# Starting a two-block kernel with the values of unnormalized x, weight parts made ahead, bias rows spread in pieces

## The chip, the cores and the metric

The kernel runs on one core of a Trainium2 chip, as one program. The metric is the device time of one execution in microseconds. Three runs of the kernel before gave a median of 2781.17 us (2778.04 to 2782.7).

## What is computed

Two blocks follow each other on 256 tokens of width 1024, all in float32. The first is a hybrid mixer and a gated feed-forward network; the second has four layers (gated linear attention, a convolution, grouped attention, gated linear attention), each with modulation by two condition vectors and a feed-forward network. Only the first block's mixer is touched. Cut to what matters:

```
h = rmsnorm(x, norm1_w)          # x * rsqrt(mean(x*x) + eps) * norm1_w, per token
q, k, v, z, xbc, dt, gates = split(h @ w_in)
attn = windowed attention of q, k, v in three dilations, 24 heads,
       logits + a bias row per head (looked up by distance)
ssm  = state-space scan of conv(xbc), with dt and z, then a norm
h2   = (gate0 * (attn @ w_attn) + gate1 * (ssm @ w_ssm)) @ w_out
```

A norm multiplies every token by one number and every channel by another. The channel factor can be put on x before a projection and the token factor on its result.

## The kernel before, in words

Activations are kept with channels on the 128 partitions and tokens along the row. A matrix product in float32 is made of three faster ones (`mm3`, L453): each operand is split into a high part, a rounded copy, and a low part, the rest; high times high, high times low and low times high are added up in PSUM.

Weights come from one packed array in units (`Unit`, L424). A unit has parts of 128 x 1024 values, 512 KB each. For each part SP issues a load into `wraw` (three buffers), ScalarE casts it into `whi` and VectorE subtracts to `wlo` (five buffers each; both on L435). A unit of the values has four parts, a unit of keys, queries or the SSM two. `fm2` (L594) takes a unit and runs its 48 matmuls into one PSUM bank of the tag `pl` (three buffers); the tag `pa` has five.

The instructions are traced in the order of the Python code, and a scheduler of the framework orders each engine's queue when the program is built: an instruction that was traced later may be put earlier where it expects its inputs to be ready. Each queue then runs in that fixed order. `order(a, b)` adds an edge that keeps a behind b. SP, ScalarE and GpSimd issue the DMAs from their own queues.

The start (L1762 to 1770) warms TensorE on zeros, loads x in four pieces on the queues of SP and ScalarE, then the whole vector table (`vec`) and the constants (`cst`). `block1` (L889) then runs in this order: `norm_plain` (L538) sums the squares, makes the per-token factor (`rstd_of`, L488) and the scaled h in two parts; `head_bias` (L606) multiplies one-hots by the bias table, writes the rows to DRAM and returns `spread` (L622), which writes each row 128 times to `ud` in DRAM, in three DMAs of eight heads each on ScalarE's queue; `decays` (L629) makes the step sizes dt; `attention` (L669) makes values in three units, keys in six and, between the heads' pairs, queries in six (`proj`, L684). `spread` is called after the first unit of keys; `load_bias` (L701) reads each head's bias from `ud` over GpSimd's queue. `conditions` (L1772) loads the condition vectors and takes their silu, traced before the first logits. `ssd` (L782) runs the SSM in four groups; each takes five units by `fm2` (B and C, two of x, two of z), with a convolution (`conv`, L789) on VectorE between them.

Of the kernel before, what the change touches and what calls it, by code (L numbers as in the profile page):

```python
# [138 lines left out]
NVEC = _o  # L139

# [7 lines left out]
CSTS = [("ident", 128), ("ones", 128), ("tri", 128), ("cumf", 128), ("cumb", 128), ("maskf", 128), ("maskb", 64),  # L148
# [8 lines left out]
def _constants():  # L157
# [8 lines left out]
    put("ones", 1.0)  # L166
# [162 lines left out]
def tile_blocks(ctx: ExitStack, tc: tile.TileContext, x, cx, wpk, wmod, vecd, rowd, cstd, hotd, g2d, out,  # L329
# [58 lines left out]
    ident, ones = cc("ident"), cc("ones")  # L388
# [35 lines left out]
    class Unit:  # L424
        def __init__(self, name, i, after=()):
            off, self.kt, self.cw = plan[name][i]
            n = self.kt * self.cw
            self.parts = []
            last_unit[0] = self
            for h in range(n // 1024):  # L430
                raw = glob.tile([P, 1024], FT, name="wraw", tag="wraw", bufs=WRAW)
                self.dma = nc.sync.dma_start(raw, bass.AP(tensor=wpk.tensor, offset=wpk.offset + off + h * 1024, ap=[[n, P], [1, 1024]])).ins
                hi = glob.tile([P, 1024], FR, name="whi", tag="whi", bufs=WHI)
                lo = glob.tile([P, 1024], FR, name="wlo", tag="wlo", bufs=WHI)
                i = A.copy(hi, raw).ins, V.tensor_tensor(lo, raw, hi, op=OP.subtract).ins  # L435
                for a, b in zip(i, after[h] if after and isinstance(after[0], tuple) else after):
                    if b is not None:
                        order(a, b)
                self.parts.append((hi, lo))
# [154 lines left out]
    def fm2(name, i, a, outer="f", after=()):  # L594


        w = Unit(name, i, after)
        ps = PL()
        order_ = [(k, f) for k in range(w.kt) for f in range(2)]
        if outer == "f":  # L600
            order_.sort(key=lambda x: x[1])
        for k, f in order_:
            mm3(ps, ps.t[:, f * 256:f * 256 + 256], w.at(k, f), a.at(k), k == w.kt - 1 and f == 1)
        return ps.t.rearrange("p (f t) -> p f t", f=2)

    def head_bias(pool):  # L606

        ud = dr.tile([24, P, BW], FT, name="ud")
        wide = []
        for g in range(N_DIL):  # L610
            hot = pool("hot", [33, BW])
            nc.sync.dma_start(hot, hotd[:, g * BW:(g + 1) * BW])
            o = VOFF["rel"][0] + g * HPG
            ps = PA()
            T.matmul(ps.t[0:HPG, :BW], vec[0:33, o:o + HPG], hot, start=True, stop=True)
            u = pool("u", [HPG, BW])
            order(A.copy(u, ps.t[0:HPG, :BW]).ins, norm_end[0])
            rows = dr.tile([HPG, BW], FT, name=f"rows{g}")
            nc.scalar.dma_start(rows, u)
            wide.append((ud[g * HPG:(g + 1) * HPG], rows))  # L620
# [8 lines left out]
    def decays(pool, h):  # L629

        w = Unit("dt", 0)
        ps = PL()
        for k in range(KD8):
            mm3(ps, ps.t[:, :256], w.at(k, 0), h.at(k), k == KD8 - 1)
        xd = glob.tile([32, 256], FT, name="xd")
# [33 lines left out]
    def attention(pool, h, ud, spread, ab, late):  # L669

        pool.tags(k=6, bt=4, L1=4, L0=4, P1=2, P0=2, dt=5)
        vt = [[O2([P, 512]) for _ in range(3)] for _ in range(2)]
        for i in range(3):
            w = Unit("v", i, () if i else norm_end)
            ps = [PL() for _ in range(2)]
            for k0 in range(0, KD8, 2):
                for t in range(2):
                    for k in (k0, k0 + 1):
                        mm3(ps[t], ps[t].t, h.at(k, t * P, P), w.row(k), k == KD8 - 1)
            for t in range(2):  # L680
                A.copy(vt[t][i], ps[t].t)
        kf, qf = [], []

        def proj(name, dst, i):  # L684
            ps = fm2(name, i, h)
            t = O2([P, 2, 256]) if name == "q" else pool(name, [P, 2, 256])
            A.copy(t, ps)
# [73 lines left out]
        conditions(lambda: pool("P1", [P, 512], pad=[P, 768]))  # L761
# [20 lines left out]
    def ssd(pool, h, lad, dt_tm, la_tm, ys):  # L782
# [22 lines left out]
        for g in range(SSM_G):  # L805
# [6 lines left out]
            conv(fm2(f"s{g}", 0, h), 0, bc, (16 + g, 20 + g))  # L812
            for i in range(2):
                conv(fm2(f"s{g}", 1 + i, h), 1 + i, xs[i], (g * 4 + 2 * i, g * 4 + 2 * i + 1))
            zt = []
            for i in range(2):
                ps = fm2(f"s{g}", 3 + i, h)
# [70 lines left out]

    def block1(early, final):  # L889
        with Pool("b1a") as pool:  # L890
            pool.tags(ct=10, hot=3, u=3)
            h = norm_plain(pool, lambda k: X[:, k, 0:256], "norm1", 256)
# [3 lines left out]
        with Pool("b1b") as pool:  # L896
            attention(pool, h, ud, spread, ab, late)
# [871 lines left out]
    nc.scalar.dma_start(vec, vecd[:, 0:NVEC])  # L1769
    nc.sync.dma_start(cst, cstd[:, 0:COFF["cos"][0]])  # L1770

    def conditions(th_):  # L1772

        o = ROFF["c"][0]
        nc.scalar.dma_start(cs.rearrange("p s d -> p (s d)"), bass.AP(tensor=rowd.tensor, offset=rowd.offset + o, ap=[[0, P], [1, 2 * D]]))
# [76 lines left out]
```

## Time and profile before

| | us |
|---|---|
| median of three runs | 2781.17 |
| the profiled execution | 2785.1 |
| its span | 2783.3 |
| TensorE busy | 2715.7 |
| VectorE busy | 2154.4 |
| ScalarE busy | 1275.4 |

The span is what the instruction records of the profiled execution cover; its own time is 1.8 us longer. PE is TensorE's matmuls, PEld its weight loads, DVE VectorE, ACT ScalarE, POOL GpSimd, SP the queue that issues loads; a name with a q, such as ACTq, is an engine's sequencer, which issues DMAs and waits. A row of the timeline gives the start, the length (from the first to the last of merged instructions), what it is with the tiles it writes and reads, and in brackets the idle time before it and what ended that.

### The profile page before, as it was taken

To read this page: it belongs to the slowest core of one execution; us is meant where nothing else is said; L and a number is where in the kernel's file an instruction comes from. 1 tells how busy PE (TensorE), PEld (TensorE's weight loads), DVE (VectorE), ACT (ScalarE), POOL (GpSimd) and SP (SyncE) were. 2 spreads that over 40 slices of the span, in tenths; PEclk is the share of its full clock that TensorE was granted. 3 is DMA by queue.
4 is the path that set the end of the run, shared out by engine and by line. 5 is a ranking of instruction groups with operands and counts; after the bars stand their busy time and mean duration, and the time that the engine had idled before them with its cause. 6 is when DMAs were issued, how large, how long until landed. Compare 5 with 4: busy or idle time off the path is not lost. (4 is left out here: it accounts for less than half of the span.)

```text
span 2783.3 us, 44045 instructions
## 1 busy us (share of the span) xinstructions
PE 2715.7 (98%) x17170; PEld 2380.8 (86%) x17170; DVE 2154.4 (77%) x3698; ACT 1275.4 (46%) x2227; POOL 213.2 (8%) x210
## 2 busy tenths in 40 slices
PE   9999999999999999999989999999999999999999
PEld 6899999999888888888668888897698888988999
DVE  6558896977785999657989997587699964754766
ACT  5456754445544423227654233245443323464543
POOL 0001000000000000003920000004600000000000
PEclk9999999999999999999999999999999999999999
DMA  7644465863443566333435663321156633222554
GB/s 236 224 149 135 151 231 204 288 208 122 143 151 103 170 210 208 118 96 97 133 111 177 209 208 121 102 84 46 47 166 212 211 114 100 89 82 84 176 184 141
DMA packets 122093, 420.40 MB, mean 151 GB/s; under 512 B 13201, under 2 KB 20108, under 8 KB 121756
## 3 DMA queue, kind: packets, MB, share of 16 engines
q1 hardware_dynamic: 114788, 402.45, 44.6%
q0 software_dynamic: 2080, 7.37, 0.8%
q10 hardware_dynamic: 5016, 7.76, 0.8%
q8 instruction: 135, 2.21, 0.3%
q14 instruction: 74, 0.61, 0.1%
HBM read 407.67 MB, written 5.84 MB: 149 GB/s over the span
## 5 line engine op out<-in xcount | busy, mean ns | idle before, releaser
L456 PE MATMUL pl<-hA,whi 128*128 128x256 f32 (+1 forms) x5056 | 1148.2, 321 | 6.4 <-ACT whi L435 1.7
L435 ACT CAST whi<-wraw 128x1024 fp32r<-128x1024 f32 x553 | 578.9, 1050 | 916.3 <-PE pl L456 409.6
L456 PEld LDWEIGHTS pl<-hA,whi 128*128 128x128 f32 x5056 | 848.1, 192 | 83.5 <-ACT whi L435 3.6
L435 DVE TENSOR_TENSOR wlo<-wraw,whi 128x1024 fp32r<-128x1024 f32 x553 | 680.8, 1234 | 291.0 <-ACT whi L435 288.4
L456 PE MATMUL pl<-hA,wlo 128*128 128x256 f32 (+1 forms) x2528 | 807.9, 321 | 8.2 <-DVE wlo L435 8.2
L456 PE MATMUL pa<-oA,whi 128*128 128x512 f32 (+1 forms) x2592 | 640.0, 338 | 0.0
L456 PEld LDWEIGHTS pl<-hA,wlo 128*128 128x128 f32 x2528 | 483.3, 192 | 47.7 <-DVE wlo L435 10.9
L456 PEld LDWEIGHTS pa<-oA,whi 128*128 128x128 f32 x2592 | 447.4, 190 | 52.6
L564 DVE SCALAR_TENSOR_TENSOR mj<-mr,cs 128x1024 bf16<-128x1024 f32 x384 | 468.8, 1221 | 12.0 <-DMA mr<-in_wmod_dram 8.2
L456 PE MATMUL pa<-oA,wlo 128*128 128x512 f32 (+1 forms) x1296 | 438.0, 338 | 0.0
L1097 DVE SCALAR_TENSOR_TENSOR X<-pa,MOD,X 128x256 f32<-128x256 f32 x448 | 198.5, 479 | 106.7 <-PE pa L456 104.8
L456 PEld LDWEIGHTS pa<-oA,wlo 128*128 128x128 f32 x1296 | 245.9, 190 | 26.4
L456 PE MATMUL pl<-oA,whi 128*128 128x256 f32 (+1 forms) x1088 | 218.4, 300 | 11.3 <-ACT oA L459 11.3
L456 PE MATMUL pl<-whi,hA 128*128 128x256 f32 (+1 forms) x992 | 228.8, 321 | 0.2
L456 PEld LDWEIGHTS pl<-oA,whi 128*128 128x128 f32 x1088 | 175.8, 194 | 18.4 <-ACT oA L459 12.2
L456 PEld LDWEIGHTS pl<-whi,hA 128*128 128x128 f32 x992 | 169.4, 196 | 12.8 <-DVE hA L1015 0.7
L456 PE MATMUL pl<-oA,wlo 128*128 128x256 f32 (+1 forms) x544 | 161.8, 299 | 0.0
L456 PE MATMUL pl<-wlo,hA 128*128 128x256 f32 (+1 forms) x496 | 158.7, 320 | 0.0
L459 ACT CAST oA<-ct 128x256 fp32r<-128x256 f32 (+1 forms) x178 | 89.1, 506 | 149.1 <-DVE ct L1137 138.2
L1712 POOL TENSOR_SCALAR pr<-pr,s 128x512 f32<-128x512 f32 (+1 forms) x64 | 78.3, 1241 | 501.8 <-DVE s L1710 501.5
L460 DVE TENSOR_TENSOR oA<-ct,oA 128x256 fp32r<-128x256 f32 (+1 forms) x178 | 96.6, 546 | 22.5 <-ACT oA L459 22.2
L456 PEld LDWEIGHTS pl<-oA,wlo 128*128 128x128 f32 x544 | 105.1, 194 | 2.5
(302 smaller groups left out, 2577.9 us busy)
## 6 DMA issues: line engine op xcount, KB each, us to landing
wraw<-in_wpk_dram SPq DMA_DIRECT2D x553, 512.0 KB, 4.0
mr<-in_wmod_dram SPq DMA_DIRECT2D x192, 512.0 KB, 4.3
U<-u SPq DMA_DIRECT2D x24, 265.5 KB, 4.9
ud<-rows ACTq DMA_DIRECT2D x3, 1536.0 KB
la<-lad POOLq DMA_DIRECT2D x8, 512.0 KB, 4.8
bt<-ud POOLq DMA_DIRECT2D x8, 384.0 KB, 5.9
U<-u SPq DMA_DIRECT2D x4, 273.5 KB, 5.0
U<-u SPq DMA_DIRECT2D x4, 269.5 KB
```

The lines of the kernel that those rows point to most:

```text
L435: i = A.copy(hi, raw).ins, V.tensor_tensor(lo, raw, hi, op=OP.subtract).ins
L456: T.matmul(o, l, r, start=ps.start(), stop=stop and i == 2)
L459: A.copy(hi, src)
L460: return V.tensor_tensor(lo, src, hi, op=OP.subtract).ins
L564: m = V.scalar_tensor_tensor(pool("mj", [P, D], BF), raw, 0.5, cs[:, s], op0=OP.mult, op1=OP.mult, accum_out=MOD[:, l, f, s:s + 1]).ins
L1097: V.scalar_tensor_tensor(X[:, k, c], ps, MOD[:, l, g + k, s:s + 1], X[:, k, c], op0=OP.mult, op1=OP.add)
L1712: G.tensor_scalar(pr, pr, dn[:, a:a + 1], None, op0=OP.mult)
```

## The change

The first block begins with a new function, `first_values`. It multiplies x by the norm's channel weight alone and projects the values from that; squares are summed beside it, and the per-token factor is put on the values when they leave PSUM. The normalized h is made afterwards, for dt, keys, queries and the rest. The first three weight parts are asked for ahead of the constants, and only the head of the vector table comes before them. `fm2` takes the next unit's name and traces its loads, casts and subtractions (`ahead`) before the result of the present unit is evicted; this is used for values, dt, keys, queries and the SSM's units. `spread` writes two heads of each dilation at a time: after key units 0 and 2 and at the head pairs 0 and 1. The conditions move to head pair 2. The ones matrix is filled on the chip.

```diff
-CSTS = [("ident", 128), ("ones", 128), ("tri", 128), ("cumf", 128), ("cumb", 128), ("maskf", 128), ("maskb", 64),
+CSTS = [("ident", 128), ("tri", 128), ("cumf", 128), ("cumb", 128), ("maskf", 128), ("maskb", 64),
...
+    ones = glob.tile([P, P], FT, name="ones")
+    V.memset(ones, 1.0)
...
+            for h in range(self.kt * self.cw // 1024 if whole else 0):
+                self.fetch()
+                self.cut(after[h] if after and isinstance(after[0], tuple) else after)
...
+    def ahead(name, i):
+        ready[name, i] = Unit(name, i)
...
-        w = Unit(name, i, after)
+        w = ready.pop((name, i), None) or Unit(name, i, after)
...
+        if nxt:
+            ahead(*nxt)
         return ps.t.rearrange("p (f t) -> p f t", f=2)
...
-        def spread(after):
-            for dst, rows in wide:
-                i = nc.scalar.dma_start(dst, rows[:, None, :].to_broadcast([HPG, P, BW])).ins
+        def spread(p, after):
+            for g, rows in enumerate(allrows):
+                i = nc.scalar.dma_start(ud[g * HPG + 2 * p:g * HPG + 2 * p + 2],
+                                        rows[2 * p:2 * p + 2, None, :].to_broadcast([2, P, BW])).ins
                 order(i, after)
...
         for i in range(6):
-            proj("k", kf, i)
-            if i == 0:
-                spread(last_unit[0].dma)
+            proj("k", kf, i, ("k", i + 1) if i < 5 else ("q", 0))
+            if i in (0, 2):
+                spread(i // 2, copied[0])
...
-        conditions(lambda: pool("P1", [P, 512], pad=[P, 768]))
...
-                proj("q", qf, done)
+                proj("q", qf, done, ("q", done + 1) if done < 5 else None)
                 done += 1
+            if qb and p < 2:
+                spread(p + 2, copied[0])
+            if qb and p == 2:
+                conditions(lambda: pool("P1", [P, 512], pad=[P, 768]), copied[0])
...
+            after_ = lambda i: (f"s{g}", i + 1) if i < 4 else (f"s{g + 1}", 0) if g + 1 < SSM_G else None
+            conv(fm2(f"s{g}", 0, h, nxt=after_(0)), 0, bc, (16 + g, 20 + g))
...
+    def first_values(pool):
+        x_ = lambda k: X[:, k, 0:256]
+        xg, h = Acts(256, "hA"), Acts(256, "hA")
+        vt = [[O2([P, 512]) for _ in range(3)] for _ in range(2)]
+        w = Unit("v", 0, whole=False)
+        for _ in range(3):
+            w.fetch()
+        nc.sync.dma_start(cst, cstd[:, 0:COFF["cos"][0]])
+        nc.sync.dma_start(vec[:, NV0:NVEC], vecd[:, NV0:NVEC])
+        acc = pool("ct", [P, 256], pad=[P, 512])
+
+        def part(w, ps, k0):
+            for t in range(2):
+                for k in (k0, k0 + 1):
+                    mm3(ps[t], ps[t].t, xg.at(k, t * P, P), w.row(k), k == KD8 - 1)
+
+        banks = [PA(), PA()]
+        for k0 in range(0, KD8, 2):
+            if k0 == 2:
+                w.fetch()
+            for k in (k0, k0 + 1):
+                hi, lo = xg.at(k)
+                A.activation(hi, x_(k), AF.Copy, scale=vv("norm1", k))
+                V.scalar_tensor_tensor(lo, x_(k), vv("norm1", k), hi, op0=OP.mult, op1=OP.subtract)
+            w.cut()
+            part(w, banks, k0)
+            for k in (k0, k0 + 1):
+                if k == 0:
+                    act(acc, x_(k), AF.Square)
+                    continue
+                q = ct(pool, 256)
+                act(q, x_(k), AF.Square)
+                V.tensor_tensor(acc, acc, q, op=OP.add)
+        ps = PL().t
+        T.matmul(ps[:, 0:256], ones, acc, start=True, stop=True)
+        for t in range(2):
+            T.matmul(ps[:, 256 + t:257 + t], acc[:, t * P:t * P + P], ones[:, 0:1], start=True, stop=True)
+        rt = rstd_small(ps[:, 256:258], D, 2)
+        r = rstd_of(pool, ps[:, 0:256], D, 256)
+        for i in range(3):
+            if i:
+                w = ready.pop(("v", i))
+                banks = [PA(), PA()]
+                for k0 in range(0, KD8, 2):
+                    part(w, banks, k0)
+            ahead(*(("v", i + 1) if i < 2 else ("dt", 0)))
+            for t in range(2):
+                A.activation(vt[t][i], banks[t].t, AF.Copy, scale=rt[:, t:t + 1])
+            if i == 0:
+                for k in range(KD8):
+                    f = ct(pool, 256)
+                    V.scalar_tensor_tensor(f, x_(k), vv("norm1", k), r, op0=OP.mult, op1=OP.mult)
+                    last = split(f, *h.at(k))
+                hold[:] = [last]
+        return h, vt
...
-            h = norm_plain(pool, lambda k: X[:, k, 0:256], "norm1", 256)
+            h, vt = first_values(pool)
...
-    nc.scalar.dma_start(vec, vecd[:, 0:NVEC])
-    nc.sync.dma_start(cst, cstd[:, 0:COFF["cos"][0]])
+    nc.scalar.dma_start(vec[:, 0:NV0], vecd[:, 0:NV0])
```

## Rows read from the trace of the kernel before

**Rows 1.** The page, part 1: busy time and share of each engine.
```profile
PE 2715.7 (98%) x17170; PEld 2380.8 (86%) x17170; DVE 2154.4 (77%) x3698; ACT 1275.4 (46%) x2227; POOL 213.2 (8%) x210
```

**Rows 2.** Stretches: busy PE, PEld, DVE, ACT, POOL; granted clock, DMA share, GB/s.
```profile
0.00:56.29 56.29, 52.31 (x214) 37.19 (x215) 37.70 (x69) 30.54 (x51) 0.90 (x5) 0.94 0.70 231
...
56.29:106.60 50.31, 47.15 (x385) 46.26 (x383) 20.63 (x17) 21.11 (x24) 3.09 (x4) 1.00 0.78 269
...
106.60:118.00 11.40, 6.19 (x37) 5.22 (x36) 8.00 (x12) 5.53 (x8) 0.00 (x0) 0.71 0.64 213
...
240.00:380.00 140.00, 129.40 (x1055) 122.46 (x1054) 126.30 (x228) 99.35 (x196) 12.38 (x10) 0.95 0.43 141
```

**Rows 3.** Timeline of the first 20 us: start, length, instruction, idle before.
```profile
4.96 2.69 ACT L408 ACTIVATE ct<-X 128x256 f32<-128x256 f32 x8 [2.94 <-DMA X<-in_x_dram]
...
6.31 53.33 SPq L432 DMA_DIRECT2D wraw<-in_wpk_dram  x18
...
8.90 1.15 PE L523 MATMUL pa<-ct,cst 128*128 128x256 f32 x2 [2.05 <-DVE ct L528]
...
11.56 1.05 ACT L435 CAST whi<-wraw 128x1024 fp32r<-128x1024 f32 x1 [0.15 <-DMA wraw<-in_wpk_dram]
...
12.64 1.23 DVE L435 TENSOR_TENSOR wlo<-wraw,whi 128x1024 fp32r<-128x1024 f32 x1 [0.77 <-ACT whi L435]
...
15.07 2.10 PE L615 MATMUL pa<-hot,vec 33*8 33x384 f32 x6
...
18.06 0.38 PE L456 MATMUL pl<-hA,whi 128*128 128x256 f32 x1 [0.89 <-ACT hA L459]
```

**Rows 4.** Two stretches of 2 us, columns as in rows 2.
```profile
4.00:6.00 2.00, 2.00 (x7) 0.75 (x6) 0.29 (x1) 1.04 (x4) 0.00 (x0) 1.00 1.06 374
...
20.00:22.00 2.00, 2.00 (x9) 1.81 (x8) 2.00 (x6) 1.70 (x4) 0.00 (x0) 0.50 0.03 7
```

**Rows 5.** Timeline of the bias spreads, of the first keys and bias loads.
```profile
44.75 0.75 ACTq L624 DMA_DIRECT2D ud<-rows  x1
...
50.11 1.21 ACTq L624 DMA_DIRECT2D ud<-rows  x1
...
56.57 5.76 ACTq L624 DMA_DIRECT2D ud<-rows  x1
...
62.37 0.58 ACT L687 COPY k<-pl 128x512 f32<-128x512 f32 x1 [4.34 <-PE pl L456]
...
63.95 0.50 PE L456 MATMUL pl<-hA,whi 128*128 128x256 f32 x2 [1.71 <-ACT whi L435]
...
85.51 3.09 POOL L704 DMA_DIRECT2D bt<-ud  x4 [34.07 <-PE pl L456]
```

**Rows 6.** Waits of SP's queue, 72 to 120 us: total, times, longest.
```profile
SPq L432 <- DMA ud<-rows: 7.3, 1, 7.3
```

**Rows 7.** Timeline before the first logits of attention.
```profile
111.49 1.04 ACT L435 CAST whi<-wraw 128x1024 fp32r<-128x1024 f32 x1 [1.21 <-DMA wraw<-in_wpk_dram]
...
113.07 1.23 PE L720 MATMUL pl<-k,oA 64*128 64x256 f32 x4 [3.74 <-ACT oA L687]
```

**Rows 8.** TensorE's waits, 240 to 380 us: total, times, longest.
```profile
PE pa L837 <- DVE hA L803: 3.9, 4, 1.8
...
PE pl L456 <- DVE wlo L435: 3.8, 3, 1.7
```

**Rows 9.** The conditions' tile (min, median, max), then the table load in the timeline.
```profile
L404 ACT ACTIVATE P<-cs x4: 616/623/629, 29.6 to 35.9; 128x512 f32<-128x512 f32 x4
...
L1780 DVE SCALAR_TENSOR_TENSOR cs<-P,cs x4: 666/672/673, 31.2 to 40.5; 128x512 f32<-128x512 f32 x4
...
DMA to landing us min/median/max: 7.5/7.5/7.5
...
27.37 1.28 ACT L400 ACT_TABLE_LOAD   x1
...
28.67 1.05 ACT L435 CAST whi<-wraw 128x1024 fp32r<-128x1024 f32 x1
```

More of the change, by code (lines that the diff above doesn't have):

```diff
@@ L386, in cc @@
         return cst[:, o:o + w]
-    ident, ones = cc("ident"), cc("ones")
+    ident = cc("ident")
+    ones = glob.tile([P, P], FT, name="ones")
+    V.memset(ones, 1.0)
     tab = {"cur": None, "load": None, "since": []}
@@ L424, in tile_blocks, with __init__, fetch, cut @@
     class Unit:
[L425 to L428, printed above, removed]
+        def __init__(self, name, i, after=(), whole=True):
+            self.off, self.kt, self.cw = plan[name][i]
+            self.parts, self.raws = [], []
             last_unit[0] = self
[L430 to L439, printed above, removed]
+            for h in range(self.kt * self.cw // 1024 if whole else 0):
+                self.fetch()
+                self.cut(after[h] if after and isinstance(after[0], tuple) else after)
+        def fetch(self):
+            n, h = self.kt * self.cw, len(self.parts) + len(self.raws)
+            raw = glob.tile([P, 1024], FT, name="wraw", tag="wraw", bufs=WRAW)
+            self.dma = nc.sync.dma_start(raw, bass.AP(tensor=wpk.tensor, offset=wpk.offset + self.off + h * 1024, ap=[[n, P], [1, 1024]])).ins
+            self.raws.append(raw)
+        def cut(self, after=()):
+            raw = self.raws.pop(0)
+            hi = glob.tile([P, 1024], FR, name="whi", tag="whi", bufs=WHI)
+            lo = glob.tile([P, 1024], FR, name="wlo", tag="wlo", bufs=WHI)
+            i = A.copy(hi, raw).ins, V.tensor_tensor(lo, raw, hi, op=OP.subtract).ins
+            for a, b in zip(i, after):
+                if b is not None:
+                    order(a, b)
+            self.parts.append((hi, lo))
         def cols(self, o, n):
@@ L634, in decays @@
             mm3(ps, ps.t[:, :256], w.at(k, 0), h.at(k), k == KD8 - 1)
+        ahead("k", 0)
         xd = glob.tile([32, 256], FT, name="xd")
@@ L667, in decay_sums, with attention, proj @@
         V.tensor_copy(tmv, ps.t[:, 0:128])
-    def attention(pool, h, ud, spread, ab, late):
+    def attention(pool, h, vt, ud, spread, ab, late):
         pool.tags(k=6, bt=4, L1=4, L0=4, P1=2, P0=2, dt=5)
[L672 to L681, printed above, removed]
         kf, qf = [], []
-        def proj(name, dst, i):
-            ps = fm2(name, i, h)
+        copied = []
+        def proj(name, dst, i, nxt):
+            ps = fm2(name, i, h, nxt=nxt)
             t = O2([P, 2, 256]) if name == "q" else pool(name, [P, 2, 256])
-            A.copy(t, ps)
+            copied[:] = [A.copy(t, ps).ins]
             dst.append(t)
         for i in range(6):
-            proj("k", kf, i)
-            if i == 0:
-                spread(last_unit[0].dma)
+            proj("k", kf, i, ("k", i + 1) if i < 5 else ("q", 0))
+            if i in (0, 2):
+                spread(i // 2, copied[0])
             if i == 3:
@@ L896, in block1 @@
         with Pool("b1b") as pool:
-            attention(pool, h, ud, spread, ab, late)
+            attention(pool, h, vt, ud, spread, ab, late)
         with Pool("b1c") as pool:
```

25 lines of the change are left out of this document (15 added, 10 removed).

## The prediction, made before the result was known

> **What bounds the kernel now.** I read the page's busy times first: TensorE is busy for 98% of the span [rows 1], so a gain has to come from stretches where it idles, waits or runs slowly. The table of stretches then splits the part that the diff touches into the times before 56.29, to 106.6, to 118 and from 240 to 380 us [rows 2]. TensorE is full between and behind these stretches, so I count what is saved in one of them one to one at the end.
>
> The first stretch ends at 56.29 us, where the values are complete and the keys begin. The timeline shows that no projection runs before 18.06 us [rows 3]: TensorE warms up on zeros, sums the squares and waits for the scaled activations. The first weights are asked for at 6.31 us and are cast at 11.56 us, so they are waiting when the norm ends. From 18.06 to 56.29 TensorE never idles for long, 38.2 us of values and step sizes, a few of them at the lower clock: 20 to 22 us shows a granted clock of 0.50, the 1.2 GHz level [rows 4]. What is late here is the activation, not the weights.
>
> In the second stretch 50.31 us hold 47.15 us of work: 3.2 us are lost [rows 2]. The timeline puts 1.71 us of that at 63.95 us, a wait for a cast of weights [rows 5]. ScalarE had sat idle for 4.34 us until 62.37: the row puts that down to the matmuls that the copy of key unit 0 waits for, but the issue of the third bias spread also held its queue for 5.76 us from 56.57, and the next cast stands behind both.
>
> The third stretch is the worst: 11.40 us with 6.19 us busy, at a mean granted clock of 0.71 [rows 2]. TensorE waits 3.74 us until 113.07 for the copy of query unit 1, which stands on ScalarE behind a cast at 111.49 that itself waited 1.21 us for its DMA [rows 7]. The weights were late because SP's queue stood 7.3 us behind a spread that had not landed [rows 6]; the spreads land about 85.5 us, when the first bias load starts [rows 5].
>
> From 240 to 380 us, in the SSM, VectorE is busy 126.3 of 140 us and TensorE 129.4 [rows 2]. TensorE's waits there are 3.9 us for the convolution and 3.8 us for the low parts of weights, both on VectorE [rows 8].
>
> **The values first.** The queues are passed as follows. On SP three weight parts move ahead of the 416 KB constants, of the rest of the vector table (now on SP) and of the bias one-hots. On ScalarE's queue only eleven columns of the table remain behind x, and the 1 MB of conditions leaves the start. So the first weights queue behind x alone. At 374 GB/s [rows 4] x (1 MB) and a 512 KB part need about 4.2 us; x has begun to land by 4.96 us [rows 3], and I estimate the first part at about 7.2 us. A cast (1.05) and a subtraction (1.23) later [rows 3], the second matmul can go: TensorE flows from about 9.5 us. Bounds: 8.0 us, if the part lands with x, and 13.8 us, if it lands at 11.5 as before. I take 9.5, since less lies ahead in the queues.
>
> The stream then takes the old 38.2 us. The loss at the lower clock stays in it, since TensorE again starts after an idle gap. New in it are works that ran before 18.06 us under the norm's wait: six one-hot matmuls, 2.10 us, and sums of squares, half of 1.15 us plus two small ones [rows 3], together 3.2 us. Keys begin at 9.5 + 38.2 + 3.2 = 50.9 us instead of 56.29: **5.4 us gained**. It would be 8.5 us if these hid, and 1 us at the late bound. The scaled copies cost ScalarE 8 activations of about 0.34 us (the squares' row) [rows 3] and VectorE 8 products, a quarter of a subtraction's columns each, by an estimate from the 1.23 us at most 0.5; with the first unit's four subtractions and seven adds VectorE has about 12 us of work in a unit that takes TensorE longer at its first pace, so I cost them at nothing. If that cover goes, the loss is 2 us. The norm's chain and h are hidden by value units 1 and 2; late next would be h for the step sizes. The evictions now carry a scale, which changes no count.
>
> **Spreads in four pieces.** Same bytes, twelve issues in place of three, two batches under the keys and two in attention, each behind a copy. Each carries a quarter of the rows. By the 1.21 us of the second old issue [rows 5] a batch holds ScalarE's queue for at most 3.6 us; by a quarter of that, 0.9 us. I take about 1 us, because the long issue stood behind two spreads still moving; ScalarE is 42% busy under the keys (21.11 of 50.31), so it is hidden. Queued behind an issue are casts and copies, and TensorE waits for these, with some units made ahead as cover. SP's 7.3 us wait should go, since a small piece lands long before its turn on SP's queue comes again.
>
> The Trainium skill, DMA: Bandwidth & Descriptors (Rules for kernel authors), speaks against this: it wants a megabyte or more in one transfer and gives 75% of peak from there. If the pieces of 384 KB lost a quarter of their rate, the 41 us from 44.75 to 85.51 would become some 55 us of sharing, and the waits would stay as they are in the first rival. No row shows a spread of that size.
>
> **Units made ahead, in keys and queries.** The casts of the next unit stand ahead of the copy of this one. That helps at 63.95 us and takes nothing off any engine; 2.5 of the 3.2 us go. At 107 us the same order puts copies behind casts, so it helps only if weights are on time. With the 7.3 us wait gone and half the spread bytes moved behind 107 us I expect that. The loss there is 11.40 - 6.19 = 5.2 us of idling and about 2.5 us of work at the lower clock; I take **6 of 7.7**. Both together 8.5 us, between 0 and 10.9.
>
> **SSM.** Subtractions pass ahead of the convolution's work. Of 3.8 us of waits, and at most 7 us of time at the lower clock (0.95 mean over 140 us means 14 us at half speed [rows 2]), the best is 9.5 us. But VectorE's work is unchanged and fills 126.3 us, and each subtraction set before a convolution (1.23 us) can lengthen the other wait, four of them: 4.9 us lost. I take 2.5 us gained, nearer to the wait's own size, as only part of it turns into speed.
>
> **Conditions in attention.** Four tanh of 0.62 us, four products of 0.67 us, a table load of 1.28 us [rows 9], a 1 MB load and six spread issues come into the softmaxes. The load took 7.5 us to land. If ScalarE stands in line for it, that is the loss; if it hides, nothing. I take 1.5 us lost. After the table load a cast follows with no visible gap (27.37 + 1.28, then 28.67 us). The Trainium skill, ScalarE: Activation LUTs (What ACT_TABLE_LOAD costs), adds a drain, for 2.66 us per switch; by it the loss would be 2.9 us. The row decides, at 1.28.
>
> **Sum.** 5.4 + 8.5 + 2.5 - 1.5 = 14.9 us. The profiled execution took 2785.1 us (span 2783.3), 3.9 us above the median of the runs; from it the sum gives 2770.2, and from the median 2781.2 it gives **2766 us**.
>
> **Rivals.** First, casts still block the copies: the weights stay late, since the keys still need their bytes beside the spreads, and only the front stays. 5.4 - 1.5 = 3.9 us, 2777 us. For it: the order of casts ahead of copies is written in now. Against: the one long wait on SP's queue has a name that the change shortens. Chance 0.15.
>
> Second, slower: ScalarE's queue blocked by issues. If each of the twelve took the 5.76 us of the third, a batch would hold casts for 17.3 us; three parts ahead cover three times about 2.9 us (47.15 us of work over 16 parts), 8.7 us. Four batches lose 34 us, less the 14.9: 19 us more, 2800 us. It turns into a loss above (8.7 + 3.7) / 3 = 4.1 us per issue. For it: the one row of 5.76. Against: 0.75 and 1.21 us on the two others [rows 5], with four times the rows. Chance 0.10.
>
> Third, the change does not do what it says: the values do not begin early, because the first scaled copies or parts land at the late bound, and the start gives 1 us. 1 + 8.5 + 2.5 - 1.5 = 10.5 us, 2771 us. Against: x alone lies ahead of the weights. Chance 0.05.
>
> **The numbers.** My own case has 0.70. Its range runs from 2754 (8.5 + 10.9 + 9.5 - 1.5 = 27.4 us) to 2775, where the SSM gives back. The range to 2779 takes in the first rival and leaves out the second and the tails. What a measurement of this kernel can tell from no change is about 0.2%, 5.6 us. Faster by more: 0.68 from my case, 0.05 from the first rival, 0.04 from the third: 0.77. Within: 0.02, 0.09 and 0.01: 0.12. Slower: 0.11.
>
> **What would show it.** A projection matmul before 10 us and a first key matmul near 51 us bear out the front. No 7 us wait of SP for a spread, no TensorE gap over 2 us before the first logits, and query copies within 2 us of their matmuls bear out the middle. Issues of spreads above 4 us would make it the second rival. In the SSM the waits for low parts shrink; if those for the convolution grow as much, that term is zero. The forecast is wrong if keys begin after 54 us, if ScalarE stands behind the conditions' load for more than 3 us, or if what is saved at the start returns as idling before 120 us.

## The result, and the profile after

The changed kernel takes **2826.17 us** (median of 4 runs, 2820.20 to 2830.59), the kernel before beside it 2781.51 us (2778.04 to 2782.70): ratio 1.0153, 95% interval 1.0142 to 1.0165 (the two medians by themselves give 1.0161). It is 44.7 us slower; 2766 us were forecast. The profiled execution spans 2828.8 us. Two lines of its page, the busy times and the spread issues:

```profile
PE 2719.4 (96%) x17156; PEld 2385.4 (84%) x17156; DVE 2158.7 (76%) x3712; ACT 1277.8 (45%) x2237; POOL 212.4 (8%) x210
...
ud<-rows ACTq DMA_DIRECT2D x12, 384.0 KB
```

TensorE's share fell from 98% [rows 1] to 96%: it has been made to wait. To find where, I read two events that every version has: the first gate activation, with which the work behind attention begins, and the first scaled x of the feed-forward's norm, which stands behind the SSM and the mixer's last projections. The same two rows, of the kernel before and then of the changed one (groups of tile X: min, median and max duration in ns, first and last start):

```profile
L404 ACT ACTIVATE X<-pl x4: 591/594/597, 179.8 to 205.7; 128x512 f32<-128x512 f32 x4
...
L545 DVE SCALAR_TENSOR_TENSOR ct<-X,vec,ct x8: 480/481/486, 466.8 to 472.0; 128x256 f32<-128x256 f32 x8
```

```profile
L406 ACT ACTIVATE X<-pl x4: 591/594/597, 221.8 to 247.7; 128x512 f32<-128x512 f32 x4
...
L557 DVE SCALAR_TENSOR_TENSOR ct<-X,vec,ct x8: 479/484/491, 511.9 to 517.0; 128x256 f32<-128x256 f32 x8
```

The gate comes 42.0 us later, the norm 45.1 us later, the end of the span 45.5 us. So 42 us were lost before the gate, about 3 more in the SSM, and next to nothing behind. I call the first time below "the gate" and the distance between the two "the SSM's length": 287.0 us before, 290.1 after.

**The start** came out near the forecast. Three rows of the changed kernel's timeline (start, length, instruction, idle before):

```profile
8.20 1.04 ACT L447 CAST whi<-wraw 128x1024 fp32r<-128x1024 f32 x1 [1.41 <-DMA wraw<-in_wpk_dram]
...
9.71 1.22 PE L468 MATMUL pa<-whi,hA 128*128 128x512 f32 x2 [2.42 <-ACT hA L931]
...
50.12 0.40 PE L468 MATMUL pl<-hA,whi 128*128 128x256 f32 x2
```

Projections flow from 9.71 us. The 24 matmuls of the step sizes end and the keys begin at about 50.1 us, 6.2 us earlier than in the profiled execution of before [rows 2].

**Then ScalarE stands still.** The same timeline, ScalarE and its queue, from the first spread on:

```profile
56.79 8.15 ACTq L645 DMA_DIRECT2D ud<-rows  x2
...
64.98 7.76 ACTq L645 DMA_DIRECT2D ud<-rows  x1
...
72.78 0.58 ACT L701 COPY k<-pl 128x512 f32<-128x512 f32 x1 [14.51 <-issue]
...
72.91 8.86 ACTq L645 DMA_DIRECT2D ud<-rows  x1
...
81.80 17.40 ACTq L645 DMA_DIRECT2D ud<-rows  x2
...
99.24 1.99 ACT L447 CAST whi<-wraw 128x1024 fp32r<-128x1024 f32 x2 [24.44 <-issue]
...
146.08 0.94 ACT L406 ACTIVATE L<-L,s 128x768 f32<-128x768 f32 x1 [11.09 <-issue]
...
171.29 0.93 ACT L406 ACTIVATE L<-L,s 128x768 f32<-128x768 f32 x1 [16.57 <-issue]
```

The queue is busy issuing, not computing: 15.9 us for the first batch, 26.3 us for the second (8.86 + 17.40). All twelve issues of the kernel (shortest, median and longest in ns, first and last start):

```profile
L645 ACTq DMA_DIRECT2D ud<-rows x12: 579/7721/10202, 56.8 to 161.6; - x12
```

Each time, the row behind it has its idle time put down to "issue", the word for an engine that waited for nothing the profile shows; here it is the issue standing ahead of it in the same queue. The first batch holds a key copy, the second the casts of weights, the two in attention the exponentials of the softmaxes. TensorE pays for it, in its timeline and in stretches (PE, PEld, DVE, ACT, POOL busy; granted clock, DMA share, GB/s), three of six with the sum of the six, then the sum over the same time in the kernel before:

```profile
100.33 0.80 PE L468 MATMUL pl<-hA,whi 128*128 128x256 f32 x2 [19.64 <-ACT whi L447]
```

```profile
80.00:100.00 20.00, 0.69 (x4) 0.39 (x2) 0.00 (x0) 0.76 (x1) 1.58 (x2) 0.59 0.24 85
...
140.00:160.00 20.00, 15.41 (x112) 14.13 (x111) 4.80 (x12) 4.47 (x11) 0.00 (x0) 0.83 0.14 51
160.00:180.00 20.00, 13.02 (x113) 10.66 (x113) 11.07 (x20) 8.43 (x17) 1.51 (x2) 0.83 0.31 100
sum 120.00, PE 76.90 PEld 70.76 DVE 43.48 ACT 30.65 POOL 5.30; mean PE 12.82 PEld 11.79 DVE 7.25 ACT 5.11 POOL 0.88
```

```profile
sum 120.00, PE 110.35 PEld 99.79 DVE 69.43 ACT 56.78 POOL 7.21; mean PE 18.39 PEld 16.63 DVE 11.57 ACT 9.46 POOL 1.20
```

Between 80 and 100 us TensorE does 0.69 us of work. In the 120 us from 60 to 180 it is busy 76.9 us, where the kernel before was busy 110.35; and the mean granted clock of the six stretches lies between 0.59 and 0.87, the higher of its two levels mixed with the lower.

The last two columns point to the cause: while ScalarE's queue stands, the DMA engines are busy for a share of only 0.14 to 0.31 and move little. The DMA view of 60 to 100 us, in slices of one microsecond, of the changed kernel:

```profile
DMA  7882111121111111492111111111111897111111
GB/s 177 181 313 85 54 52 65 49 79 51 50 49 49 52 49 51 161 344 104 57 47 49 49 52 49 49 52 49 49 52 49 143 409 290 49 51 52 51 49 49
```

Whenever a spread piece moves alone, it moves at some 50 GB/s, mostly 49 to 52. From 84 to 91 us no other queue moves anything (packets, MB, share of the time of 16 engines; q10 carries the spreads):

```profile
q10 hardware_dynamic: 230, 0.35, 13.2%
```

Two engines of sixteen would be 12.5%. At 50 GB/s a piece of 384 KB needs 7.9 us, and 7.7 us is the median length of an issue, by the row of the twelve above. A piece has two heads as the outermost dimension of its source and destination; the whole spread of before had eight.

### The profile page after: what moved, and what is told of

It is laid out like the page before. It is cut to its first block, busy times and chain, and to the rows that moved or that the text cites. A ratio compares the mean times of both kernels' runs of the same rounds, so it can differ in the third digit from the quotient of the medians.

```text
span 2828.8 us, 44045 instructions
## 1 busy us (share of the span) xinstructions
PE 2719.4 (96%) x17156; PEld 2385.4 (84%) x17156; DVE 2158.7 (76%) x3712; ACT 1277.8 (45%) x2237; POOL 212.4 (8%) x210
## 4 chain that ended last, share of the span: by engine, by line
PE 75%; DVE 10%; DMA 5%; POOL 3%; ACT 3%; issue 3%; ACTq 2%; SPq 0%; POOLq 0%; DVEq 0%
PE pl L468 44%; PE pa L468 24%; DMA wraw<-in_wpk_dram 3%; DVE wlo L447 2%; ACTq L645 2%; POOL oA L1568 2%; ACT whi L447 1%; POOL pr L1788 1%; PE pa L1813 1%; DVE c L817 1%; DVE ct L1089 1%; PE pa L1452 1%; DVE mj L576 1%; DMA mr<-in_wmod_dram 1%; DVE hA L1091 1%
## 5 line engine op out<-in xcount | busy, mean ns | idle before, releaser
L468 PEld LDWEIGHTS pl<-hA,wlo 128*128 128x128 f32 x2528 | 484.1, 192 | 47.5 <-DVE wlo L447 11.4
L468 PE MATMUL pl<-whi,hA 128*128 128x256 f32 (+1 forms) x896 | 197.9, 313 | 0.2
L468 PEld LDWEIGHTS pl<-whi,hA 128*128 128x128 f32 x896 | 151.1, 196 | 9.3 <-DVE hA L1091 0.7
L468 PE MATMUL pl<-wlo,hA 128*128 128x256 f32 (+1 forms) x448 | 139.7, 313 | 0.0
```

The costliest lines, as they stand in the source:

```text
L468: T.matmul(o, l, r, start=ps.start(), stop=stop and i == 2)
```

## The experiments

**Theory A**: a spread runs on as many DMA engines as its outermost dimension has rows, up to sixteen. A piece carries a quarter of the bytes on a quarter of the engines, takes as long as the whole did, and there are four times as many; each later issue holds ScalarE's queue until an earlier one is through. **Rivals**: B, the place or the number of the pieces blocks the queue, whatever their shape; C, a transfer of 384 KB is slow because it is small; D, not named in the expectations, units made ahead turn the casts into the wait; and for the smaller terms, the ones named in each expectation.

**sixteen**: the change, with the rows outermost instead of the heads, so that each piece has 128 outermost rows. Same bytes, same places.

```diff
-i = nc.scalar.dma_start(ud[g * HPG + 2 * p:g * HPG + 2 * p + 2],
-                        rows[2 * p:2 * p + 2, None, :].to_broadcast([2, P, BW])).ins
+i = nc.scalar.dma_start(ud[g * HPG + 2 * p:g * HPG + 2 * p + 2].rearrange("h p w -> p h w"),
+                        rows[None, 2 * p:2 * p + 2, :].to_broadcast([P, 2, BW])).ins
```

> The changed kernel with one edit: the pieces of the bias spread are written with the 128 copies as the outermost dimension instead of the 2 heads; same bytes, places and number of issues. Theory A (a piece with an outermost dimension of 2 runs on two of the sixteen DMA engines, so it takes 7.7 us and holds ScalarE's queue): issues fall under 1.5 us, the idle time of ScalarE put down to issue (over 60 us in the changed kernel) is gone, and the time is 2766 us (2758 to 2776), below the kernel before. Theory B (it is the number of issues and their place, before casts and copies on ScalarE's queue): the gaps stay and the time stays above 2800 us. Theory C (pieces of 384 KB are slow because they are small): issues stay above 4 us, time above 2800 us.

Measured: 2770.61 us (2769.35 to 2771.90), ratio to before 0.9955 [0.9940, 0.9969]. The groups of its spreads and of tile X:

```profile
L645 ACTq DMA_DIRECT2D ud<-rows x12: 537/634/1018, 57.8 to 111.5; - x12
```

```profile
L406 ACT ACTIVATE X<-pl x4: 576/592/594, 164.6 to 190.5; 128x512 f32<-128x512 f32 x4
...
L557 DVE SCALAR_TENSOR_TENSOR ct<-X,vec,ct x8: 479/480/485, 453.8 to 458.9; 128x256 f32<-128x256 f32 x8
```

One edit is worth 55.6 us by the medians. Issues fall from a median of 7.7 to 0.63 us and the gate from 221.8 to 164.6: 57 us, more than the 42.0 lost there. Twelve pieces of the same size in the same places, behind the same copies, with the same units ahead: B, C and D fall as causes of the loss. The 120 us in which TensorE was busy 76.9 us now hold this (sum of the same six stretches):

```profile
sum 120.00, PE 118.28 PEld 109.01 DVE 80.71 ACT 68.28 POOL 8.98; mean PE 19.71 PEld 18.17 DVE 13.45 ACT 11.38 POOL 1.50
```

**oldspread**: the change, with the three whole eight-head spreads in one batch behind key unit 0.

```diff
-for g, rows in enumerate(allrows):
-    i = nc.scalar.dma_start(ud[g * HPG + 2 * p:g * HPG + 2 * p + 2],
-                            rows[2 * p:2 * p + 2, None, :].to_broadcast([2, P, BW])).ins
+for g, rows in enumerate(allrows if p == 0 else ()):
+    i = nc.scalar.dma_start(ud[g * HPG:(g + 1) * HPG],
+                            rows[:, None, :].to_broadcast([HPG, P, BW])).ins
```

> The changed kernel with the spread as before: three DMAs of eight heads after key unit 0, all else changed. Theory A: each of these has 192 KB per engine on eight engines, as a piece has on two, so three such waits remain where there were twelve; the loss is a quarter or less, and the front's 6 us show: 2780 us (2768 to 2792). Theory B (places of the issues): the three stand at one place under the keys and the attention is free of them: 2770 to 2785. If the time stays above 2815, the cause is not the spread.

Measured: 2784.92 us, ratio 1.0004 [0.9994, 1.0013]: what the start gains, spreads bunched in this way take back. The time alone fits A and B alike; the rows tell them apart. The spread group, the rate of its DMA view from 60 to 100 us, and its queue from 68 to 74 us, where hardly anything else moves:

```profile
L645 ACTq DMA_DIRECT2D ud<-rows x3: 760/7771/8596, 57.2 to 66.6; - x3
```

```profile
GB/s 206 218 197 334 222 218 201 214 216 200 203 202 199 200 203 200 200 203 249 380 381 347 366 300 202 211 243 347 266 253 345 409 310 214 105 331 187 33 225 221
```

```profile
q10 hardware_dynamic: 780, 1.19, 52.3%
```

Eight heads outermost: 199 to 203 GB/s, four times the 50 of two heads, and four times the share of the engines. The second and third issues take 7.8 and 8.6 us, and the key copy behind them waits 15.8 us; each is as long as a piece's in the changed kernel, though each carries four times the bytes: 1536 KB at 200 GB/s is 7.9 us again.

**four**: the change, with pieces of four heads behind key units 0 and 2.

```diff
-i = nc.scalar.dma_start(ud[g * HPG + 2 * p:g * HPG + 2 * p + 2],
-                        rows[2 * p:2 * p + 2, None, :].to_broadcast([2, P, BW])).ins
+i = nc.scalar.dma_start(ud[g * HPG + 4 * p:g * HPG + 4 * p + 4],
+                        rows[4 * p:4 * p + 4, None, :].to_broadcast([4, P, BW])).ins
...
-if qb and p < 2:
-    spread(p + 2, copied[0])
```

> The changed kernel with pieces of four heads at two places, after key units 0 and 2: six DMAs with an outermost dimension of 4, 768 KB each. Theory A (as many engines as the outermost dimension): four engines move some 100 GB/s, 192 KB on each as in every version so far, so an issue that waits for one before it takes 7.7 us again, and six of them cost about half of what twelve did: 2795 us (2785 to 2810), rows of about 100 GB/s under the keys. Theory C (size of a transfer): a piece of twice the size is faster per byte by some tens of per cent, not by two.

Measured: 2802.87 us in one run. Its spread group, the rates from 60 to 100 us, and the queue of the spreads from 68 to 75 us:

```profile
L645 ACTq DMA_DIRECT2D ud<-rows x6: 727/8306/11519, 57.6 to 88.3; - x6
```

```profile
GB/s 227 280 215 305 192 112 99 115 100 124 101 100 100 100 101 182 313 202 107 97 98 103 100 100 101 100 100 101 100 139 201 391 356 378 331 98 101 101 100 101
```

```profile
q10 hardware_dynamic: 456, 0.69, 26.3%
```

Alone, a piece of four heads moves at 97 to 103 GB/s. So 2, 4 and 8 outermost rows give 50, 100 and 200 GB/s, 25 each, and take 13.2, 26.3 and 52.3% of the time of sixteen engines, as much as 2.1, 4.2 and 8.4 engines have. The packets are of 1.5 KB in all three (MB by packets), so it is not their size. The medians of the issues lie at 7.7 to 8.3 us in all three; what differs is how many there are.

**before2**: the kernel before, with each spread cut into four two-head pieces, all twelve at the old place. Nothing else of the change.

```diff
-for dst, rows in wide:
-    i = nc.scalar.dma_start(dst, rows[:, None, :].to_broadcast([HPG, P, BW])).ins
+for p in range(4):
+    for dst, rows in wide:
+        i = nc.scalar.dma_start(dst[2 * p:2 * p + 2], rows[2 * p:2 * p + 2, None, :].to_broadcast([2, P, BW])).ins
```

> The kernel before with one edit: each of the three spreads cut into four pieces of two heads, all twelve at the old place under the first keys, outermost dimension 2. Theory A: twelve issues of some 7.7 us at one place, about 90 us in which ScalarE can cast little; with what is made ahead hidden, 2781 + 50 = 2830 us (2810 to 2860). Theory B (the places in attention cost the time): under 2800 us, since nothing stands in attention. Theory C (small transfers): slower as well, by the same count.

Measured: 2849.86 us in one run, 66.7 us more than the kernel before beside it (2783.14). The spread group and the longest wait of TensorE up to 400 us:

```profile
L625 ACTq DMA_DIRECT2D ud<-rows x12: 719/7736/9612, 45.2 to 128.7; - x12
```

```profile
PE pl L456 <- ACT whi L435: 74.9, 1, 74.9
```

The cut by itself brings the whole loss into a kernel that has none of the other parts. In the changed kernel it costs less; I put that down to the pieces being spread out, which no run parts from the units made ahead.

**before16**: the kernel before, its three whole spreads with the rows outermost.

```diff
-i = nc.scalar.dma_start(dst, rows[:, None, :].to_broadcast([HPG, P, BW])).ins
+i = nc.scalar.dma_start(dst.rearrange("h p w -> p h w"), rows[None, :, :].to_broadcast([P, HPG, BW])).ins
```

> The kernel before with one edit: its three spreads of eight heads written with the 128 copies outermost. Theory A: three issues under 1.5 us (one took 5.76), SP's wait of 7.3 us behind a spread is gone, and with it the late weights at 107 us: 2773 us (2768 to 2779). Theory B or C (engines don't matter, bytes and places do): 2781 within 0.2%.

Measured: 2778.39 us, ratio 0.9983 [0.9973, 0.9992]. The issues fall to 0.54, 0.54 and 0.66 us (before 0.75, 1.21 and 5.76 [rows 5]), and SP's 7.3 us wait [rows 6] is gone. The first key matmul and TensorE's wait before the first logits:

```profile
52.72 0.40 PE L456 MATMUL pl<-hA,whi 128*128 128x256 f32 x2
...
108.69 1.23 PE L720 MATMUL pl<-k,oA 64*128 64x256 f32 x4 [3.77 <-ACT oA L687]
```

The gate comes at 175.7, 4.1 us earlier, but its keys had begun at 52.72 us already, at a granted clock of 1.00 over the first 20 us against 0.89 in the kernel before, which is 3.6 us that no spread gave. Of the 4.8 us in the medians the profile so places 0.5 between the first keys and the gate; where the rest comes from is open. So by the profile the shape of the spreads cost the kernel before little: two of its three issues found the queue nearly free.

The second row sets a reading of the prediction right. TensorE's wait before the first logits, put down there to SP's wait for a spread, is as long without it: 3.77 us against 3.74 [rows 7]. It is there in all four kernels with whole spreads in one place (3.6 us in whole16, 6.0 in oldspread) and at most 1.4 us in all six with pieces on all engines. By these runs it goes with where the spreads' bytes move, not with that wait.

**whole16**: the change, with oldspread's three whole spreads behind key unit 0, the rows outermost.

```diff
-for g, rows in enumerate(allrows):
+for g, rows in enumerate(allrows if p == 0 else ()):
-    i = nc.scalar.dma_start(ud[g * HPG + 2 * p:g * HPG + 2 * p + 2],
-                            rows[2 * p:2 * p + 2, None, :].to_broadcast([2, P, BW])).ins
+    i = nc.scalar.dma_start(ud[g * HPG:(g + 1) * HPG].rearrange("h p w -> p h w"),
+                            rows[None, :, :].to_broadcast([P, HPG, BW])).ins
```

> The changed kernel with the spread whole again, three DMAs of eight heads after key unit 0, on sixteen engines. Theory A (what counts is the engines, not the pieces): issues under 1.5 us, time within 0.15% of the kernel with pieces on sixteen engines, 2768 to 2775. Rival (the pieces take DMA load from the keys to the attention, and that is part of the gain): 2776 to 2780.

Measured: 2782.05 us, ratio 0.9998 [0.9988, 1.0008], 11.4 us slower than sixteen by the medians, with the same bytes on the same engines: theory A alone did not expect that, and the rival had the direction, though the time lies above its range too. The spread group, TensorE's wait before the first logits, then the transfers of 60 to 100 us here and in sixteen:

```profile
L645 ACTq DMA_DIRECT2D ud<-rows x3: 660/677/6525, 56.9 to 58.3; - x3
```

```profile
PE pl L734 <- ACT oA L701: 4.0, 2, 3.6
```

```profile
q10 hardware_dynamic: 2868, 4.33, 33.5%
...
wraw<-in_wpk_dram SPq DMA_DIRECT2D x11, 512.0 KB, 8.4
```

```profile
q10 hardware_dynamic: 1571, 2.27, 16.7%
...
wraw<-in_wpk_dram SPq DMA_DIRECT2D x14, 512.0 KB, 6.4
```

The queue that carries the spreads moves 4.33 MB in these 40 us; in sixteen it is 2.27 MB, and there the weights get 14 loads at a median of 6.4 us instead of 11 at 8.4. So the cut does have worth: it takes half the bytes out of the keys' time. It needs all engines to have it. Of the 13.8 us between the two profiled executions 8.9 lie before the gate; 4.0 lie in the SSM, which has no spread, at a granted clock of 0.97 there against 0.99, and the place of the spreads does not explain those. Nor is a held issue gone with all engines: the third of the three still took 6.5 us.

**nossm** and **nokq**: sixteen without units made ahead in the SSM, and without those in keys and queries.

```diff
-conv(fm2(f"s{g}", 0, h, nxt=after_(0)), 0, bc, (16 + g, 20 + g))
+conv(fm2(f"s{g}", 0, h), 0, bc, (16 + g, 20 + g))
```

(and alike at the two other calls of the SSM); nokq:

```diff
-        ahead("k", 0)
...
-ps = fm2(name, i, h, nxt=nxt)
+ps = fm2(name, i, h)
```

> The kernel with the pieces on sixteen engines, without making units ahead in the SSM (keys, queries and values keep it). In the kernel with sixteen engines the first gate came 15.2 us earlier than in the kernel before and the feed-forward's norm only 13.1 us earlier, so the SSM lost about 2 us. Theory A (subtractions put before the convolution lengthen the SSM): the loss goes, 2768 us (2766 to 2770), 0.1% under the sixteen-engine kernel. Rival (making ahead helps the SSM, and something else costs there): 2772 us or more.

> The kernel with the pieces on sixteen engines, without making units ahead for keys and queries (values and SSM keep it). Theory A (the weights are on time now, so the order of casts and copies matters little): within 0.1% of the sixteen-engine kernel, 2769 to 2773. Rival (making ahead carries the gain under the keys, as the prediction had it with 2.5 us): 2773 to 2778.

Measured: nossm 2766.38 us (2764.79 to 2767.86), ratio 0.9942 [0.9930, 0.9954], the lowest median of this study; nokq 2770.16 us, 0.9962 [0.9949, 0.9975], the same as sixteen. The SSM as a stretch, first in sixteen, then in nossm:

```profile
199.00:454.00 255.00, 240.96 (x1971) 230.31 (x1971) 214.36 (x356) 154.27 (x274) 15.12 (x12) 0.99 0.54 180
```

```profile
199.00:447.00 248.00, 239.35 (x1970) 230.20 (x1969) 214.49 (x357) 155.06 (x274) 15.95 (x12) 0.99 0.54 185
```

The same work in 7 us less, 5.4 of them idle time of TensorE (14.0 against 8.7 us). The medians differ by 4.2 us only: nossm's profiled execution is the fastest of its five, sixteen's the second slowest of its four, and the intervals of the two ratios overlap. Against nokq, which has units ahead in the SSM and was timed beside it, the five times of nossm lie apart (at most 2767.86 against at least 2769.50). The waits moved as follows, sixteen first:

```profile
PE pl L468 <- DVE wlo L447: 4.6, 3, 2.0
PE pa L893 <- ACT ct L869: 3.3, 2, 1.9
PE pa L855 <- DVE hA L820: 2.8, 2, 1.8
...
ACT whi L447 <- DMA wraw<-in_wpk_dram: 38.2, 23, 3.6
```

```profile
PE pa L855 <- DVE hA L820: 3.7, 3, 1.8
PE pl L468 <- DVE wlo L447: 3.2, 3, 1.2
PE pa L893 <- ACT ct L869: 1.3, 1, 1.3
...
ACT whi L447 <- DMA wraw<-in_wpk_dram: 16.9, 14, 2.7
```

Made ahead, the low parts are not earlier: TensorE waits longer for them (4.6 against 3.2 us) and for the copy of the scan's state on ScalarE (3.3 against 1.3), and a little less for the convolution (2.8 against 3.7). That is 2.5 of the 5.4 us. In sixteen ScalarE stands 38.2 us before casts whose weights have not landed, in nossm 16.9, and the copy of the state stands behind such casts; that this makes the loss I read from the rows, no run isolates it. The SSM's length says the same over all kernels: 286.4 to 293.2 us in the six with units ahead there (the change, sixteen, oldspread, whole16, four, nokq), 282.2 to 287.1 in the seven without. Part of the scatter goes with the granted clock over that length: at 0.98 it is 289.5 to 290.1 us with units ahead and 287.0 and 287.1 without, at 0.99 286.4 and 289.2 against 282.2 to 284.8. So units ahead cost some 3 us there; the pairs that differ in them alone, sixteen and nossm, nokq and both (below), lie 4.2 and 2.6 us apart in the medians. What of nossm's gain over the kernel before, which runs the same SSM in 287.0 us at 0.98, belongs to the clock and what to earlier work is open.

**nofront**, **both**, **cond**: nossm with one more part changed each. nofront has the old start: the norm first, the values from its result, the tables loaded as before. both has no units ahead under keys and queries either. cond has the conditions back at their old place.

```diff
# nofront
-h, vt = first_values(pool)
+h = norm_plain(pool, lambda k: X[:, k, 0:256], "norm1", 256)
...
+vt = [[O2([P, 512]) for _ in range(3)] for _ in range(2)]
+for i in range(3):
+    w = Unit("v", i, () if i else norm_end)
...
# both: nossm's and nokq's edits together
...
# cond
-if qb and p == 2:
-    conditions(lambda: pool("P1", [P, 512], pad=[P, 768]), copied[0])
...
+conditions(lambda: pool("P1", [P, 512], pad=[P, 768]))
 load_bias(0)
```

> nossm with the old start: the norm first, then the values from its result, the tables and constants loaded at the start as before; spreads in pieces on sixteen engines, no units ahead in the SSM. Theory: the values' early begin is worth what the forecast said, since TensorE is full behind it: keys begin some 5 to 6 us later than in nossm (56 instead of 50 us) and the whole takes 2771 to 2773 us. Rival: what is won at the start is given back before the first gate activation, because the weights' transfers and not TensorE set the pace of the keys: the gate activation moves by less than 2 us and the whole takes 2765 to 2768 us.

> nossm without units made ahead in keys and queries too: what is left of the change is the early values, the pieces on sixteen engines and the conditions in attention. Theory: units ahead under keys and queries are worth nothing once the pieces hold no engine for long, so it takes what nossm took, 2765 to 2768 us. Rival: without any unit ahead a cast waits behind a copy in keys and queries, as at 63.95 us of the kernel before, and it takes 2 to 5 us more, 2769 to 2771 us.

> nossm with the conditions at the old place, ahead of the attention loop and with no order behind a copy. Theory: ScalarE's wait for their load (4.5 us in the changed kernel) stands among the softmaxes and costs 2 to 4 us; at the old place the load is on its way while keys are computed and it takes 2762 to 2765 us. Rival: there the 1 MB load competes with weights and spreads, and what is saved in attention is lost in the keys: 2766 us or more.

Measured: nofront 2773.89 us, 0.9967 [0.9954, 0.9980]; both 2767.52 us, 0.9949 [0.9934, 0.9964]; cond 2769.38 us, 0.9958 [0.9941, 0.9975]. In the run called both the theory held: its time cannot be told from that of nossm. For nofront, the gate rows of nossm and then of nofront:

```profile
L406 ACT ACTIVATE X<-pl x4: 572/593/594, 164.2 to 190.1; 128x512 f32<-128x512 f32 x4
```

```profile
L406 ACT ACTIVATE X<-pl x4: 574/589/594, 172.8 to 198.7; 128x512 f32<-128x512 f32 x4
```

8.6 us at the gate, 7.5 us in the medians; the early start is not given back later. Its last value copy stands at 59.48 us, 3.0 us later than that of the kernel before, so some of this is that kernel's own delay, and by this run the start's worth lies between 5.6 and 8.6 us. In cond the theory missed. The first key matmul:

```profile
52.41 0.40 PE L468 MATMUL pl<-hA,whi 128*128 128x256 f32 x2
```

The megabyte is asked for at 14.33 us, beside the weights of the values, TensorE waits 1.48 us for a low part at 37.37, and the keys begin 2.8 us later than in nossm (49.61) and 1.5 us later than in any other kernel with this start; the gate comes 3.3 us later than in nossm, at 167.5. The rival had the sign, but the loss lies in the values and not in the keys. By these profiled executions the conditions' new place is the better one; the two times alone, with overlapping intervals, do not show it.

## Why the prediction was wrong

The outcome is the second rival, ScalarE's queue blocked by issues, which had a chance of 0.10 and lay outside the range.

**The step that failed** is the price of an issue: "Each carries a quarter of the rows. By the 1.21 us of the second old issue [rows 5] a batch holds ScalarE's queue for at most 3.6 us; by a quarter of that, 0.9 us. I take about 1 us". Measured: 15.9, 26.3, 12.5 and 24.8 us for the four batches, 79.5 us together. Two errors are in it. I divided by rows, as if a piece had the whole's engines; it has a quarter of them, so no piece is shorter than the whole. And I took the two cheap rows for the price and the 5.76 us for an accident of two spreads still moving. It was the other way round. By an estimate from the 7.9 us that a spread takes alone, the first had little left to move when the second was issued 5.4 us later, and the third had nearly all of the second ahead of it. An issue that stands behind others is held for about a transfer, and in a batch of three most of them do. Even the upper bound of 3.6 us was therefore a bound from the wrong rows; the 5.76 us of [rows 5] times three, 17.3, was the near one (19.9 on average).

The Trainium skill, DMA: Bandwidth & Descriptors (Rules for kernel authors), states in its row on using all 16 engines that an outermost dimension smaller than 16 confines the whole transfer to that many engines at most. The 50, 100 and 200 GB/s at 2, 4 and 8 agree with it. I had weighed only the rule of the same page of the Trainium skill on a megabyte per transfer, which speaks against small pieces for another reason. No run here tests that one by itself: on all engines, pieces of 384 KB beat whole spreads of 1536 KB by 11.4 us, but they stand in other places too.

The terms, one by one:

- **Start, forecast 5.4 us gained: the number came out, in part by luck.** Values from 9.71 us (forecast 9.5), keys at 50.1 (50.9), 6.2 us gained; by nofront 5.6 to 8.6. But the first part was there at 8.20 us, not at 7.2, and the first matmul waited for the scaled x, which stood behind that part's cast on ScalarE, not for a subtraction. And before16 has the old start with its keys at 52.72 us, at the full clock: against that the new one, 49.6 to 50.9 in the eight kernels that have it unaltered, gains 1.8 to 3.1 us. How often the old start gets that clock no run shows.
- **Keys and queries, forecast 8.5 us gained: 48 us lost** (42.0 at the gate and the 6.2 won ahead of it). With the pieces on all engines the gate comes 15.2 us earlier than before; from the first key matmul on, 113.7 us in place of 123.5, 9.8 us less. So the gain was there to be had, in the size forecast, but not by the causes named: nokq, without units ahead, takes 114.1, and before16, without SP's wait for a spread, 123.0. Pieces in four places on all engines are what the kernels with the gain have in common. SP's wait, forecast gone, is 5.5 us in the changed kernel.
- **SSM, forecast 2.5 us gained: 3.1 us lost.** The sign was wrong, the bound of 4.9 us lost held, but not for the reason given: by sixteen and nossm the wait for the convolution did not grow, the waits for the low parts and for ScalarE's copy of the state did. The best case of 9.5 us does not follow from its terms either (3.8 and 7 make 10.8); that moves the end of the range by 1.3 us and changes nothing here.
- **Conditions, forecast 1.5 us lost.** ScalarE waits 4.5 us for their load in the changed kernel, more than the 3 us named as the limit, and 1.2 us in nossm, where the queue flows. Against the old place the move is rather worth some 3 us, by the profile of cond.

6.2 gained, 48.2 and 3.1 lost make 45.1 us, the shift of the norm, beside the 44.7 of the medians. The rival had the place and the mechanism right and came to 2800 us, 26 short: the price per batch was near (17.3 against 19.9), but the 8.7 us of cover that it took off each batch was not there in full. The four batches held the queue for 79.5 us, those of sixteen for 8.0; 58.0 of these 71.5 us reached the gate, counted from the first key matmul, so by this estimate some 3.4 us per batch were covered. Why so little I read from the rows, no run isolates it: the key copy and the exponentials of the softmaxes stand in the same queue as the casts, and nothing of them is made ahead.

## What to carry to other kernels

Before cutting a transfer, look at its outermost dimension: with 8 rows and fewer, as here, cutting along it took engines away in step with the bytes, and nothing got shorter. The price of an issue is read from the row where it stands behind another, not from the one that found the queue free, and issues of slow transfers do not belong in the queue of an engine whose casts others wait for (no run tried another queue). Work made ahead is not free: in the SSM, with VectorE busy for nine tenths of the stretch [rows 2], it cost some 3 us, and under keys and queries it brought nothing. The version with the lowest median is nossm, ahead of both kernels: 2766.38 us, with the early start, the pieces with rows outermost, and the SSM as it was.

## What the runs showed of the hardware that was not expected

- A transfer within device memory moved at 25 GB/s per outermost row: 49 to 52 with 2, 97 to 103 with 4, 199 to 203 with 8, with 2.1, 4.2 and 8.4 engines' worth of time in use. In sixteen, with 128 outermost rows, all traffic together reaches 417 GB/s in a slice.
- An issue is no fixed cost. In the changed kernel the same instruction took 0.58 us at the shortest and 7.7 us in the median, most of the twelve behind their like: about the time that one of those transfers takes alone; by what resource it is held, no row shows.
- Three whole spreads in one batch did no better on all engines than on eight: oldspread and whole16 take the same time within their intervals. In the one ScalarE waits 15.8 us behind the issues; in the other weights land in 8.4 us where they take 6.4 in sixteen.
